# Memory sums, feed-forward preparation, key eviction and side work rearranged in a one-core decoder step

## The chip, the cores and the metric

The kernel runs on one core of a Trainium2 chip. The metric is the device time of one execution in microseconds; the kernel before takes 2075.16 us, the median of three runs.

## The reference, cut to what matters

One layer of a decoder for 1024 prompt tokens and 8 sample tokens (one for each of 8 requests). The 1032 columns run together through the dense products; only attention treats them apart.

```python
x = x + merged @ w_o                                    # conv and sparse attention branches
# memory cross-attention, 4 heads of 256; prompt: 256 memory tokens, samples: cached memory
q = rms_norm(x, g_mem) @ w_mq
p = softmax(q @ mem_k.T * 256 ** -0.5)
x = x + (p @ mem_v) @ w_mo
# feed-forward
h = rms_norm(x, g_ffn)
x = x + (silu(h @ w_gate) * (h @ w_up)) @ w_down
```

For the samples the memory keys and values differ from request to request, so their scores and weighted sums are no shared matrix product: each is a product with the query (or with the probabilities) and a sum over 256 elements.

## The kernel before, in words

Everything is kept transposed: channels on the 128 partitions, tokens on the free axis, as tiles of 128x1032. A float32 product is made of three fp32r products, high by high, high by low, low by high. So every operand is split: ScalarE makes the high part (a copy that rounds), and VectorE or GpSimd subtracts it to get the low part. Class `Weights` does this for the streamed weights (line 163 high, 165 low, on the engines named in `lo_engines`), `split_sb` (lines 499 and 502) for activations in SBUF; both use GpSimd unless told otherwise. Tiles come from 49 slots, handed out in the order in which they were given back. The order of instructions on each engine is the order of the program text; nothing is reordered.

`dense` (line 480) multiplies one output tile of 128 channels, 8 blocks of 9 matmuls, into three PSUM banks, in turn banks 0 to 2 and 3 to 5. `unit` (line 610) is a form with seven products instead of eight for a 2x2 block of tiles. Its weights, class `UnitWeights`, come in portions U, V, W and Y: `load` issues three DMAs, `sums` four additions on VectorE (lines 228 to 231), `high` a ScalarE copy (238) and `low` a VectorE subtraction (251). Its inputs come from `x_sums` (lines 550 to 563) and `x_last` (577, 578).

Ahead of the first unit two key tiles are computed with `dense` and copied out of PSUM on ScalarE (line 908). After the first of them the weights of unit 0 and two `x_sums` are prepared.

The memory stage. Eight `dense` steps give the eight query tiles. `evict_q` takes each out of PSUM (line 1571 on VectorE), keeps its sample columns (1572) and splits it. Beside this runs side work, one generator `mem_sample` for each of the four heads, started after query tiles 1, 3, 5 and 7. It spreads a head's sample query over the partitions (1620, 1624, 1626), forms the products with the cached keys in four parts (`products`), sends the 16 sums through DRAM (`bounce`) to come back as one row for a request, applies the softmax (1632 to 1636), spreads the probabilities (1639, 1641), forms the products with the cached values, bounces again and writes the sample columns (1649 to 1655). `bg.pump(budget)` advances the generators: each yields a cost, and a pump goes on until its budget is used or the generator yields None. Steps for TensorE are held until `bg.pe`.

Then a loop of eight steps, n = 0 to 7, does the prompt's softmax for (head, half of the queries). In its order: eviction of the output of step n-2 (`mo_evict`: ScalarE 1751 and VectorE 1752, twice), `ms_exp(n+1)` (four exponentials on ScalarE, 1703), the scores of n+2 (1684), held side work for TensorE, transposes (1717), `ms_norm(n+1)` (a reciprocal on VectorE, 1708, and four multiplications on GpSimd, 1711), the values of n-1 (1741), the high part of the transposed probabilities (ScalarE, 1723), `ms_max(n+2)` (VectorE, 1695 and 1696), their low part (VectorE, 1727), and one pump of budget 0.5. In step 6 the exponentials stand ahead of the eviction. The output product w_mo follows in `residual_gemm`, in two halves of eight `dense(4, ...)`: the first half pumps 3.5 after each and then drains the side work, the second half adds up squares and splits the result (499, 504, 1532, 1536).

The feed-forward part begins with two hidden tiles by `dense` (`FF_DIRECT`), gate and up each, with `x_sums` between, then goes on with units. Line 1872 evicts a gate tile, 1873 is its sigmoid, line 662 the multiplications, 1887 evicts an up tile.

Of the kernel before, what the change touches and what calls it, by code (L numbers as in the profile page):

```python
# [13 lines left out]
ALU = mybir.AluOpType  # L14
# [310 lines left out]
def build(tc, A):  # L325
# [28 lines left out]
    def store(dst, src, slot=None):  # L354
        def go():
            nc.sync.dma_start(dst, src)
            if slot is not None:
                S.put(slot)
        later.append(go)
# [540 lines left out]
    for g in range(2):  # L900
        ps = dense(8, h, 0.0, {k: score for k in range(8)} if g == 0 else None)
        if g == 0:
            score()
            for t in iq:
                S.put(t)
            put_pairs([ik])
        t = S.get()
        ACT.activation(full(t), ps, AF.Copy)
        V.tensor_copy(ks_new[:, g, :], t[0][:, 0:NS])
        store(A["o_kT"][g], act(t), t)  # L910
        if g == 0:
            UW.sums(0)
            UW.high(0, "U")
            UW.low(0, "U")
            for p in (2, 3):
                x_sums(h, None, p, xs[2 * p], xs[2 * p + 1])
            UW.high(0, "V")
            UW.low(0, "V")
            UW.high(0, "W")
    x_last(h)  # L920

    bias = {}
# [593 lines left out]

    x1d = dram.tile([8, 128, T], F32, name="x1d")

    def residual_gemm(src, xsrc, gi, spill, budget=0.0, hooks=None, free=True):
        xx = [load(xsrc[0])]  # L1520
        hl = []
        acc = [None]
        for kh in range(2):
            for o in range(8):
                if kh == 0 and o < 7:
                    xx.append(load(xsrc[o + 1]))
                ps = dense(4, src[4 * kh:4 * kh + 4], budget, hooks if kh == 0 and o == 0 else None)
                V.tensor_tensor(full(xx[o]), ps, full(xx[o]), op=ALU.add)  # L1528
                if kh == 1:
                    hl.append(split_sb(xx[o], scale=gain(gi, o)))  # L1530
                    s = S.get()
                    ACT.activation(s[0][:, :T], xx[o][0][:, :T], AF.Square)
                    if o == 0:
                        acc[0] = s
                    else:
                        G.tensor_tensor(acc[0][0][:, :T], acc[0][0][:, :T], s[0][:, :T], op=ALU.add)
                        S.put(s)
                    if spill is not None:
                        store(spill[o], xx[o][0][:, :T], xx[o] if free else None)
            put_pairs(src[4 * kh:4 * kh + 4])  # L1540
            bg.drain()
            budget = 0.0
        return xx, hl, acc[0]
# [19 lines left out]
    qlast = []  # L1563

    def split_q(t):
        qm.append(split_sb(t))
        S.put(t)

    def evict_q(o, ps, now=True):
# [23 lines left out]
    def products(src, hd, rows, dst):  # L1593
        for part in range(4):
            n = xjobs.index((src, hd, part))
            fetch(n + 1)
            s = xtiles.pop((src, hd, part))
            for x in range(4):
                V.tensor_tensor_reduce(out=caus, in0=s[0][:, 256 * x:256 * x + 256], in1=rows, scale=1.0, scalar=0.0,  # L1599
                                       op0=ALU.mult, op1=ALU.add, accum_out=dst[:, 4 * part + x:4 * part + x + 1])  # L1600
                if x < 3:
                    yield 0.46
            S.put(s)
            fetch(n + 1 + xahead[0])
            if part < 3:
                yield 0.46

    def bounce(hd, z, src, dst):
        def go():
            nc.sync.dma_start(bd[hd, z], src)  # L1610
            nc.sync.dma_start(dst, bd[hd, z].rearrange("(b g) j -> b (g j)", g=16))
        later.append(go)

    def mem_sample(hd):
        P = PS[:, 6 + hd // 2, 256 * (hd % 2):256 * (hd % 2) + 256]
        s = S.get()
        t = s[0]
        rep, rows, sums, p = t[:, 0:256], t[:, 256:512], t[:, 512:528], t[0:NS, 528:784]
        for x in range(2):
            V.tensor_copy(rep[:, 128 * x:128 * x + 128].rearrange("p (b r) -> p b r", r=16),  # L1620
                          qm_s[:, 2 * hd + x, :].unsqueeze(2).to_broadcast([128, NS, 16]))
        yield PE_STEP
        for x in range(2):
            PE.transpose(P[:, 128 * x:128 * x + 128], rep[:, 128 * x:128 * x + 128], ident)
        yield None
        ACT.copy(rows, P)
        yield None
        yield from products("cmk", hd, rows, sums)
        bounce(hd, 0, sums, p)
        yield None  # L1630
        m = sm[:, hd, :]
        V.reduce_max(m[:, 0:1], p, axis=AX.X)
        V.tensor_scalar(m[:, 1:2], m[:, 0:1], -SCM, None, op0=ALU.mult)
        ACT.activation(p, p, AF.Exp, bias=m[:, 1:2], scale=SCM, accum_out=m[:, 2:3])
        V.reciprocal(m[:, 3:4], m[:, 2:3])
        V.tensor_scalar(p, p, m[:, 3:4], None, op0=ALU.mult)
        yield None
        yield PE_STEP
        PE.matmul(P, sel128, p, start=True, stop=True)
        yield None  # L1640
        ACT.copy(rows, P)  # L1641
        yield None
        yield from products("cmv", hd, rows, sums)
        bounce(hd, 1, sums, p)
        yield None
        yield None
        yield PE_STEP
        for x in range(2):
            PE.transpose(P[:, 8 * x:8 * x + 8], p[:, 128 * x:128 * x + 128], ident[0:NS, 0:NS])
        yield None  # L1650
        for x in range(2):
            ACT.copy(qm[2 * hd + x][0][0][:, 0:NS], P[:, 8 * x:8 * x + 8])
        for x in range(2):
            h, l = qm[2 * hd + x]
            V.tensor_tensor(l[0][:, 0:NS], P[:, 8 * x:8 * x + 8], h[0].bitcast(F32)[:, 0:NS], op=ALU.subtract)
        S.put(s)
        done.add(hd)

    done = set()

    ps0 = dense(8, hl, hooks={7: h0})
    ps1 = dense(8, hl, hooks={5: h1})
    evict_q(0, ps0)
# [101 lines left out]
        raws.append(raw)  # L1765

    def split_mkv(z):
        (mkr if z < 2 else mvr).append(split_sb(raws[z], width=1024))
        S.put(raws[z])

    def mem_start():
# [36 lines left out]
    for n in range(8):  # L1808
        flush()
        if n == 3:  # L1810
            W.load_to(W.cur + 3)
        if n == 5:
            W.split_to(W.cur + 1)
        if n >= 2 and n != 6:
            mo_evict(n - 2)
        if n + 1 < 8:
            ms_exp(n + 1, range(4))
        if n == 6:
            mo_evict(n - 2)
        if n + 2 < 8:  # L1820
            ms_mm(n + 2, range(4))
        if n > 0:
            bg.pe()
        mt_mm(n)
        if n + 1 < 8:
            ms_norm(n + 1)
        bg.consume()
        if n == 0:
            split_mkv(2)
            split_mkv(3)  # L1830
        if n >= 1:
            mpv(n - 1)
        mt_hi(n)
        if n + 2 < 8:
            ms_max(n + 2)
        mt_lo(n)
        if n == 0:
            split_mkv(1)
        if n == 1:
            split_q(qlast.pop())  # L1840
        bg.pump(SLOT_SIDE, False)
    put_pairs(mkr)

    def finish_mem():
        mo_evict(6)
# [8 lines left out]

    W.limit = W.n - sum(len(g) for g in FF_GROUPS)
    flip[0] = 1
    xx, hl, sq = residual_gemm(qm, x1d, GFFN, x2d, 3.5, {1: finish_mem}, False)
    R, h0, h1 = norm_hooks(sq)
    Rr = R[0][:, :T]

    kept = {}
    tail = [{}]

    UW.n = A["wu"].shape[0]
    UW.load(MIX_UNITS)
    for f in FF_DIRECT:
        pg = dense(8, hl, hooks=None if f else {7: h0})
        x_sums(hl, GFFN, 2 * f, xx[4 * f], xx[4 * f + 1])
        if f == 0:
            pu = dense(8, hl, hooks={5: h1})  # L1870
        t, z = S.get(), S.get()
        V.tensor_tensor(full(t), pg, full(R), op=ALU.mult)
        ACT.activation(act(z), act(t), AF.Sigmoid)  # L1873
        mul(act(t), Rr)
        mul(act(t), act(z))
        S.put(z)
        if f == 0:
            UW.sums(MIX_UNITS)
            UW.high(MIX_UNITS, "U")
            UW.low(MIX_UNITS, "U")  # L1880
        else:
            UW.high(MIX_UNITS, "V")
            UW.low(MIX_UNITS, "V")
            UW.high(MIX_UNITS, "W")
            pu = dense(8, hl)
        x_sums(hl, GFFN, 2 * f + 1, xx[4 * f + 2], xx[4 * f + 3])
        V.tensor_tensor(full(t), pu, full(t), op=ALU.mult)  # L1887
        store(fd[f], act(t), t)
    x_last(hl)
    xx = []  # L1890
    for p in range(len(FF_DIRECT) // 2, 11):
# [11 lines left out]
        last = {}  # L1903
        if p == 10:
            def begin_down():
                W.limit = W.n
                W.load_to(W.cur + 2)
                xx.extend(load(x2d[o]) for o in range(4))
# [255 lines left out]
```

## Time and profile before

| what | value |
|---|---|
| median of three runs | 2075.16 us (2074.7 to 2077.28) |
| the profiled execution | 2075.18 us |
| its span, first to last instruction | 2073.4 us |
| TensorE matmul busy | 2037.3 us, 98% |
| VectorE busy | 1236.9 us, 60% |
| ScalarE busy | 821.6 us, 40% |
| GpSimd busy | 402.5 us, 19% |
| mean granted TensorE clock | 0.997 |

PE is TensorE, DVE VectorE, ACT ScalarE, POOL GpSimd. The profiled execution lies 1.8 us over its span, and 0.02 us over the median, so a change of the span can be put on the median as it is. TensorE is busy nearly throughout; what can be won is its waits, so the views to read are those that name what ended them.

### The profile page before, as it was taken

Reading aid. Unit: us, or ns where it says so; the run is one execution under the profiler, and the core shown is the slowest. Engines: PE = TensorE matmul, PEld = TensorE weight load, DVE = VectorE, ACT = ScalarE, POOL = GpSimd, SP = SyncE. Lnnn points to the kernel's source line nnn. Section 1 sums busy time; section 2 is a strip of 40 time slices with the busy share of each in tenths; the row PEclk is TensorE's granted clock in tenths of the full one; section 3 lists DMA queues with packets and bytes.
Section 4 is the critical chain, followed back from the end, with each engine's and each line's share of the span. In section 5 each row is a group of like instructions: output and inputs, shape, how many; then the busy total and the mean of one; then the engine's idle time right before and its main releaser. Section 6 shows DMA issues by size and latency. Waiting matters only on the chain. (4 is left out here: it accounts for less than half of the span.)

```text
span 2073.4 us, 35037 instructions
## 1 busy us (share of the span) xinstructions
PE 2037.3 (98%) x14455; PEld 1972.7 (95%) x14455; DVE 1236.9 (60%) x2174; ACT 821.6 (40%) x1326; POOL 402.5 (19%) x307
## 2 busy tenths in 40 slices
PE   8999999999999999999999999999999999999998
PEld 7999999999999987889999989999999999999997
DVE  6757677779866346852234787467677677721114
ACT  4437667775324235751122252343222222321204
POOL 0000000000001233333434352420000000274404
PEclk9999999999999999999999999999999999999999
DMA  7212312121327540053324424312221321453102
GB/s 297 87 42 83 123 42 82 62 82 52 135 93 265 179 141 29 1 194 94 131 92 148 181 101 164 116 38 73 85 78 62 103 82 62 166 192 103 51 1 82
DMA packets 79873, 217.48 MB, mean 105 GB/s; under 512 B 9690, under 2 KB 24354, under 8 KB 79714
## 3 DMA queue, kind: packets, MB, share of 16 engines
q1 hardware_dynamic: 79170, 214.73, 29.6%
q8 instruction: 113, 1.85, 0.4%
q10 hardware_dynamic: 544, 0.53, 0.1%
q14 instruction: 46, 0.38, 0.1%
HBM read 167.28 MB, written 47.94 MB: 104 GB/s over the span
## 5 line engine op out<-in xcount | busy, mean ns | idle before, releaser
L610 PE MATMUL PS<-t,t 128*128 128x258 f32 x7392 | 893.8, 283 | 7.3 <-DVE t L1887 3.2
L610 PEld LDWEIGHTS PS<-t,t 128*128 128x128 f32 x7392 | 890.8, 189 | 10.2 <-DVE t L1887 3.4
L480 PE MATMUL PS<-t,t 128*128 128x344 f32 x4824 | 769.1, 320 | 3.1 <-DVE t L165 1.3
L480 PEld LDWEIGHTS PS<-t,t 128*128 128x128 f32 x4824 | 760.7, 188 | 7.1 <-issue 1.7
L165 POOL TENSOR_TENSOR t<-t,t 128x1024 fp32r<-128x1024 f32 x66 | 160.8, 2446 | 354.9 <-ACT t L163 326.5
L251 DVE TENSOR_TENSOR t<-t,t 128x1024 fp32r<-128x1024 f32 (+1 forms) x176 | 188.8, 1086 | 6.4 <-ACT t L238 6.4
L238 ACT ACTIVATE t<-t 128x1024 fp32r<-128x1024 f32 (+1 forms) x176 | 161.7, 947 | 68.8 <-DVE t L228 60.8
L948 ACT ACTIVATE PS<-t,cand 128x1024 f32<-128x1024 f32 (+4 forms) x160 | 144.0, 900 | 55.6 <-DVE cand L955 52.5
L1967 DVE TENSOR_TENSOR t<-PS,t 128x1032 f32<-128x1032 f32 x32 | 39.5, 1233 | 163.1 <-PE PS L480 163.1
L531 POOL TENSOR_TENSOR t<-t,t 128x1032 fp32r<-128x1032 f32 x22 | 53.7, 2454 | 416.1 <-ACT t L530 401.5
L662 DVE TENSOR_TENSOR t<-t,t 128x1032 f32<-128x1032 f32 (+1 forms) x100 | 114.0, 1149 | 2.8 <-ACT t L1873 2.3
L163 ACT ACTIVATE t<-t 128x1024 fp32r<-128x1024 f32 x79 | 82.3, 1051 | 72.8 <-PE PS L480 60.9
L616 DVE TENSOR_TENSOR t<-PS,t 128x516 f32<-128x516 f32 x44 | 30.6, 695 | 108.8 <-PE PS L610 108.1
L499 ACT ACTIVATE t<-t 128x1032 fp32r<-128x1032 f32 (+2 forms) x34 | 36.0, 1067 | 142.2 <-DVE t L1511 77.1
L614 ACT COPY t<-PS 128x516 f32<-128x516 f32 x44 | 25.9, 589 | 164.8 <-PE PS L610 164.6
L1528 DVE TENSOR_TENSOR t<-PS,t 128x1032 f32<-128x1032 f32 x32 | 39.4, 1232 | 79.6 <-PE PS L480 79.6
L1599 DVE CUSTOM_DVE_ANT_0 caus<-t,t 128x256 bf16<-128x256 f32 x128 | 78.7, 615 | 10.3 <-ACT t L1641 5.3
L502 POOL TENSOR_TENSOR t<-t,t 128x1032 fp32r<-128x1032 f32 (+1 forms) x22 | 53.5, 2438 | 109.4 <-ACT t L499 91.5
L619 ACT COPY t<-PS 128x516 f32<-128x516 f32 x26 | 15.4, 592 | 144.5 <-PE PS L610 144.5
L1220 POOL TENSOR_SCALAR t<-t,ast 128x128 f32<-128x128 f32 (+7 forms) x64 | 48.1, 752 | 120.2 <-DVE ast L1219 88.0
L530 ACT ACTIVATE t<-t 128x1032 fp32r<-128x1032 f32 x40 | 41.4, 1060 | 74.1 <-PE PS L480 46.8
L1239 DVE TENSOR_TENSOR t<-PS,t 128x512 fp32r<-128x512 f32 x72 | 49.6, 688 | 32.1 <-ACT t L1235 31.4
(269 smaller groups left out, 2017.5 us busy)
## 6 DMA issues: line engine op xcount, KB each, us to landing
t<-in_ws_dram SPq DMA_DIRECT2D x86, 512.0 KB, 4.9
t<-in_wu_dram SPq DMA_DIRECT2D x44, 512.0 KB, 4.1
t<-in_wu_dram SPq DMA_DIRECT2D x88, 256.0 KB, 5.4
fd<-t SPq DMA_DIRECT2D x18, 516.0 KB
t<-fd SPq DMA_DIRECT2D x18, 516.0 KB, 11.5
t<-in_xT_dram SPq DMA_DIRECT2D x16, 516.0 KB, 8.1
t<-in_cmk_dram SPq DMA_DIRECT2D x16, 512.0 KB, 5.4
t<-in_cmv_dram SPq DMA_DIRECT2D x16, 512.0 KB, 6.0
```

The costliest lines, as they stand in the source:

```text
L163: nc.scalar.activation(h[0][:, :1024], raw[0][:, :1024], AF.Copy)
L165: eng.tensor_tensor(l[0][:, :1024], raw[0][:, :1024], h[0].bitcast(F32)[:, :1024], op=ALU.subtract)
L238: self.nc.scalar.activation(h[0][:, :w], self.raw[u][x][0][:, :w], AF.Copy)
L251: self.nc.vector.tensor_tensor(l[0][:, o:o + w], raw[0][:, :w], h[0].bitcast(F32)[:, :w], op=ALU.subtract)
L480: PE.matmul(PS[:, b + c, :CH], w, x[0][:, c * CH:(c + 1) * CH], start=(k == 0 and p == 0), stop=(k == n - 1 and p == 2))
L502: (lo or G).tensor_tensor(l[0][:, :width], src[0][:, :width], hf, op=ALU.subtract)
L531: lo.tensor_tensor(l[0][:, a:b], raw[0][:, a:b], h[0].bitcast(F32)[:, a:b], op=ALU.subtract)
L610: PE.matmul(PS[:, banks[z] + c, :HC], a, b[:, HC * c:HC * c + HC], start=j < 3 and q == 0 and p == 0 or j == 5 and q == 0 and p == 0, stop ...
L662: V.tensor_tensor(o, o, i, op=ALU.mult)
L948: ACT.activation(wide[:, :128 * (i + 1)], sc[i], AF.Sign, bias=candf[:, n:n + 1], scale=-1.0, accum_out=tval[:, n:n + 1])
L1239: V.tensor_tensor(tl[0][:, :512], PS[:, t_bank(x), :], th[0].bitcast(F32)[:, :512], op=ALU.subtract)
L1599: V.tensor_tensor_reduce(out=caus, in0=s[0][:, 256 * x:256 * x + 256], in1=rows, scale=1.0, scalar=0.0, op0=ALU.mult, op1=ALU.add, accum_o ...
```

## The change

- `products`: a part of 128x1024 was four instructions on VectorE, each a product and a sum over 256 columns. Now one VectorE multiplication makes all four products in place, and four ScalarE copies with an accumulating output make the sums. The costs yielded go from 0.46 for each of four to 0.9 for each half of a part. The sums go to `ast`, a tile of their own.
- `bounce` yields None until its two DMAs have been issued; `mem_sample` yields once more after its exponential.
- The low parts of the query tiles, of the memory keys and values, and of the weights from w_mq to the end of the softmax loop move from GpSimd to VectorE. So do the weights of the second half of w_mo and of the first feed-forward tiles; the first half of w_mo and w_down stay on GpSimd.
- In the softmax loop, from n = 1 on, there are two pumps of 0.5 at the end of a step; the last query tile is split in step 3 instead of 1.
- The portions V and W of unit 0 are prepared after both key tiles are evicted.
- The first feed-forward unit is loaded, summed and split (U, V) inside the second half of w_mo, after its tiles 2, 4, 5 and 6; W is prepared in the second hidden tile. The first up tile is evicted ahead of the second `x_sums`.

```diff
@@ first unit
-            UW.high(0, "V")
-            UW.low(0, "V")
-            UW.high(0, "W")
+    UW.high(0, "V")
+    UW.low(0, "V")
+    UW.high(0, "W")
     x_last(h)
@@ residual_gemm, second half
                         store(spill[o], xx[o][0][:, :T], xx[o] if free else None)
+                    if after and o in after:
+                        after[o]()
@@ split_q, and split_mkv likewise
-        qm.append(split_sb(t))
+        qm.append(split_sb(t, lo=V))
@@ products
+            v = s[0][:, :1024].rearrange("p (x n) -> p x n", n=256)
+            V.tensor_tensor(v, v, rows.unsqueeze(1).to_broadcast([128, 4, 256]), op=ALU.mult)
+            yield 0.9
             for x in range(4):
-                V.tensor_tensor_reduce(out=caus, in0=s[0][:, 256 * x:256 * x + 256], in1=rows, scale=1.0, scalar=0.0,
-                                       op0=ALU.mult, op1=ALU.add, accum_out=dst[:, 4 * part + x:4 * part + x + 1])
-                if x < 3:
-                    yield 0.46
+                ACT.activation(v[:, x, :], v[:, x, :], AF.Copy, accum_out=dst[:, 4 * part + x:4 * part + x + 1])
             S.put(s)
             fetch(n + 1 + xahead[0])
             if part < 3:
-                yield 0.46
+                yield 0.9
@@ bounce
         later.append(go)
+        while (hd, z) not in sent:
+            yield None
@@ softmax loop
         mt_lo(n)
+        if n:
+            bg.pump(SLOT_SIDE, False)
         if n == 0:
             split_mkv(1)
-        if n == 1:
+        if n == 3:
             split_q(qlast.pop())
         bg.pump(SLOT_SIDE, False)
@@ feed-forward
-    xx, hl, sq = residual_gemm(qm, x1d, GFFN, x2d, 3.5, {1: finish_mem}, False)
+    xx, hl, sq = residual_gemm(qm, x1d, GFFN, x2d, 3.5, {1: finish_mem}, False,
+                               {0: lows_on_vector, 2: lambda: UW.load(MIX_UNITS), 4: lambda: UW.sums(MIX_UNITS),
+                                5: lambda: first_part("U"), 6: lambda: first_part("V")})
...
         V.tensor_tensor(full(t), pu, full(t), op=ALU.mult)
+        if f == 0:
+            x_sums(hl, GFFN, 2 * f + 1, xx[4 * f + 2], xx[4 * f + 3])
```

## Rows read from the trace of the kernel before

**Rows 1.** Waits of PE, whole run: line <- releaser: us, times, longest

```profile
PE PS L1684 <- ACT t L1641: 2.1, 1, 2.1
```

**Rows 2.** Waits of PE, 1200 to 1270 us (first and last of six)

```profile
PE PS L1741 <- DVE t L1752: 1.9, 1, 1.9
...
PE PS L1717 <- POOL t L1711: 0.3, 1, 0.3
```

**Rows 3.** Windows: stretch, length, busy us (x instructions) by engine, granted clock, DMA, GB/s

```profile
1196.00:1248.00 52.00, 48.80 (x327) 43.98 (x327) 44.49 (x87) 33.65 (x93) 25.45 (x35) 1.00 0.27 101
...
1193.00:1196.00 3.00, 3.00 (x16) 3.00 (x16) 2.83 (x11) 0.00 (x0) 0.78 (x1) 0.50 0.19 76
...
1400.00:1406.00 6.00, 2.78 (x24) 2.58 (x23) 5.50 (x8) 4.41 (x9) 0.00 (x0) 1.00 0.00 0
```

**Rows 4.** Timeline before the first unit: start, us, instruction, xcount [idle before <-releaser]

```profile
166.94 1.99 ACT L238 ACTIVATE t<-t 128x1024 fp32r<-128x1024 f32 x2
...
168.84 1.01 ACT L908 ACTIVATE t<-PS 128x1032 f32<-128x1032 f32 x1
...
169.90 2.31 PE L610 MATMUL PS<-t,t 128*128 128x258 f32 x17 [2.16 <-ACT t L908]
```

**Rows 5.** Timeline, one step of the softmax loop

```profile
1223.38 3.05 PE L1684 MATMUL PS<-t,t 128*128 128x256 f32 x24
...
1225.61 1.04 ACT L1751 CAST t<-PS 128x512 fp32r<-128x512 f32 x2
...
1227.26 3.06 PE L1741 MATMUL PS<-t,t 128*128 128x512 f32 x12
...
1228.65 1.19 DVE L1695 TENSOR_REDUCE mst<-PS 128x4 f32<-128x1024 f32 x1
...
1229.88 0.44 DVE L1696 TENSOR_SCALAR mst<-mst 128x4 f32<-128x4 f32 x1
...
1230.16 2.04 PE L1684 MATMUL PS<-t,t 128*128 128x256 f32 x16
1230.22 1.21 DVE L1727 TENSOR_TENSOR t<-PS,t 128x1024 fp32r<-128x1024 f32 x1
...
1232.16 1.28 DVE L1752 TENSOR_TENSOR t<-PS,t 128x512 fp32r<-128x512 f32 x2
```

**Rows 6.** The chain of work that ended last, same step: start, us, what

```profile
1226.65 1.82 ACT t L1703 x8
```

**Rows 7.** Groups of ScalarE by shape: xcount | busy us, mean ns | idle before

```profile
L163 ACT ACTIVATE t<-t 128x1024 fp32r<-128x1024 f32 x79 | 82.3, 1051 | 72.8 <-PE PS L480 60.9 <-DMA t<-in_ws_dram 10.7 <-PE PS L610 0.7
...
L2001 ACT ACTIVATE t<-t 128x258 f32<-128x258 f32 x8 | 3.4, 422 | 8.6 <-DVE t L1996 8.6
...
L1634 ACT ACTIVATE t<-t,sm 8x256 f32<-8x256 f32 x4 | 2.0, 512 | 9.5 <-DVE sm L1633 9.5
```

**Rows 8.** Timeline, a low part of 1024 columns on VectorE

```profile
140.62 1.23 DVE L165 TENSOR_TENSOR t<-t,t 128x1024 fp32r<-128x1024 f32 x1
```

**Rows 9.** Timeline, side work on VectorE beside GpSimd

```profile
1180.58 2.47 POOL L502 TENSOR_TENSOR t<-t,t 128x1024 fp32r<-128x1024 f32 x1 [1.17 <-ACT t L499]
...
1180.87 2.48 DVE L1599 CUSTOM_DVE_ANT_0 caus<-t,t 128x256 bf16<-128x256 f32 x1
...
1183.38 0.42 DVE L1599 CUSTOM_DVE_ANT_0 caus<-t,t 128x256 bf16<-128x256 f32 x1
```

**Rows 10.** Timeline, start of the feed-forward part

```profile
1375.74 2.50 DVE L662 TENSOR_TENSOR t<-t,t 128x1032 f32<-128x1032 f32 x2 [1.13 <-ACT t L1873]
...
1381.83 0.69 DVE L550 TENSOR_TENSOR t<-t 128x516 f32<-128x516 f32 x1
...
1386.68 1.23 DVE L1887 TENSOR_TENSOR t<-PS,t 128x1032 f32<-128x1032 f32 x1
...
1388.06 11.73 PE L480 MATMUL PS<-t,t 128*128 128x344 f32 x72 [1.15 <-DVE t L1887]
...
1405.89 19.28 PE L610 MATMUL PS<-t,t 128*128 128x258 f32 x158 [3.22 <-DVE t L1887]
```

More of the change, by code (lines that the diff above doesn't have):

```diff
@@ L1517, in build, with residual_gemm @@
     x1d = dram.tile([8, 128, T], F32, name="x1d")
-    def residual_gemm(src, xsrc, gi, spill, budget=0.0, hooks=None, free=True):
+    def residual_gemm(src, xsrc, gi, spill, budget=0.0, hooks=None, free=True, after=None):
         xx = [load(xsrc[0])]
@@ L1605, in products @@
             if part < 3:
-                yield 0.46
+                yield 0.9
+    sent = []
     def bounce(hd, z, src, dst):
@@ L1611, in go @@
             nc.sync.dma_start(dst, bd[hd, z].rearrange("(b g) j -> b (g j)", g=16))
+            sent.append((hd, z))
         later.append(go)
+        while (hd, z) not in sent:
+            yield None
     def mem_sample(hd):
@@ L1617, in mem_sample @@
         t = s[0]
-        rep, rows, sums, p = t[:, 0:256], t[:, 256:512], t[:, 512:528], t[0:NS, 528:784]
+        rep, rows, p = t[:, 0:256], t[:, 256:512], t[0:NS, 528:784]
+        sums = ast.rearrange("p a b -> p (a b)")[:, 16 * (hd % 2):16 * (hd % 2) + 16]
         for x in range(2):
@@ L1628, in mem_sample @@
         yield from products("cmk", hd, rows, sums)
-        bounce(hd, 0, sums, p)
-        yield None
+        yield from bounce(hd, 0, sums, p)
         m = sm[:, hd, :]
@@ L1634, in mem_sample @@
         ACT.activation(p, p, AF.Exp, bias=m[:, 1:2], scale=SCM, accum_out=m[:, 2:3])
+        yield None
         V.reciprocal(m[:, 3:4], m[:, 2:3])
@@ L1643, in mem_sample @@
         yield from products("cmv", hd, rows, sums)
-        bounce(hd, 1, sums, p)
-        yield None
+        yield from bounce(hd, 1, sums, p)
         yield None
@@ L1659, in build @@
     done = set()
+    W.lo_engines = [V]
     ps0 = dense(8, hl, hooks={7: h0})
@@ L1767, in split_mkv @@
     def split_mkv(z):
-        (mkr if z < 2 else mvr).append(split_sb(raws[z], width=1024))
+        (mkr if z < 2 else mvr).append(split_sb(raws[z], lo=V, width=1024))
         S.put(raws[z])
@@ L1842, in build @@
     put_pairs(mkr)
+    W.lo_engines = [G]
     def finish_mem():
@@ L1856, in build, with first_part, lows_on_vector @@
     flip[0] = 1
-    xx, hl, sq = residual_gemm(qm, x1d, GFFN, x2d, 3.5, {1: finish_mem}, False)
+    UW.n = A["wu"].shape[0]
+    def first_part(x):
+        UW.high(MIX_UNITS, x)
+        UW.low(MIX_UNITS, x)
+    def lows_on_vector():
+        W.lo_engines = [V]
+    xx, hl, sq = residual_gemm(qm, x1d, GFFN, x2d, 3.5, {1: finish_mem}, False,
+                               {0: lows_on_vector, 2: lambda: UW.load(MIX_UNITS), 4: lambda: UW.sums(MIX_UNITS),
+                                5: lambda: first_part("U"), 6: lambda: first_part("V")})
     R, h0, h1 = norm_hooks(sq)
@@ L1862, in build @@
     tail = [{}]
-    UW.n = A["wu"].shape[0]
-    UW.load(MIX_UNITS)
     for f in FF_DIRECT:
@@ L1876, in build @@
         S.put(z)
[L1877 to L1883, printed above, removed]
+        if f:
             UW.high(MIX_UNITS, "W")
             pu = dense(8, hl)
-        x_sums(hl, GFFN, 2 * f + 1, xx[4 * f + 2], xx[4 * f + 3])
+            x_sums(hl, GFFN, 2 * f + 1, xx[4 * f + 2], xx[4 * f + 3])
         V.tensor_tensor(full(t), pu, full(t), op=ALU.mult)
+        if f == 0:
+            x_sums(hl, GFFN, 2 * f + 1, xx[4 * f + 2], xx[4 * f + 3])
         store(fd[f], act(t), t)
@@ L1905, in begin_down @@
             def begin_down():
+                W.lo_engines = [G]
                 W.limit = W.n
```

## The prediction, made before the changed kernel was run

> **What bounds the kernel now.** I read the busy line first: TensorE is at 98%, so the change can only move TensorE's waits. The view of waits, filtered to TensorE, says what ended them: 2.1 us ahead of the first memory scores [rows 1], 3.9 us in six waits of the softmax loop and just behind it [rows 2], 2.16 us in the first unit [rows 4], and 1.15 and 3.22 us at the start of the feed-forward part [rows 10]. That is 12.5 us, to which the windows add one stretch of 3 us at clock 0.50, 1.2 GHz, right after the 2.1 us wait [rows 3]; nearly all the gain to be had lies here. Then I read the timeline of each place, for what the late engine does before it comes to the instruction that TensorE awaits.
>
> **The change part by part.** *Key eviction.* Before the second key tile leaves PSUM (L908), ScalarE splits V and W: 1.99 us in one row [rows 4]. The second product of the unit needs the banks. Moved behind it, the two splits lie beside TensorE's second product, and V is needed one product (2.9 us) later than that. L908 comes some 1.8 us sooner: -1.8. If ScalarE's later work, the same in sum, becomes late, it is nothing: 0 to -1.9.
>
> *First feed-forward tiles.* Before, VectorE ran sums, a low part and an `x_sums` (1381.83 to 1386.68, 4.85 us) ahead of the eviction of the first up tile [rows 10]. After, that eviction follows the multiplications that end at 1378.2, and ends at 1379.4, when TensorE still works on the second gate tile, until 1386.9 (1388.06 less the wait); the 1.15 us go. Behind it VectorE has an `x_sums` (to 1384.3), a weight low part, new here (1.23 [rows 8], to 1385.5), an `x_sums` (1390.4), gate eviction 1.23, sigmoid 1.07, multiplications 2.5 (1395.2), an `x_sums` (1400.0) and the second eviction (1401.3). TensorE, 1.15 us sooner, ends its first product at about 1401.5 (1405.89 less both waits); so next to nothing is left of 3.22. Together -4.2. The moved portions (three DMAs on SP, four sums, two splits on each engine) go into the second half of w_mo, where VectorE has 2.5 us of work in a step of 5.7 and a PSUM bank waits one more step; the DMAs are issued two tiles (11 us) ahead of the sums. I cost them at nothing; if GpSimd's squares hold VectorE up there, it comes to -2.5.
>
> *Query tiles.* Without GpSimd, no instruction of VectorE stands 2.48 us instead of 0.42 beside it [rows 9]. But ScalarE now has the sums. For one sum no row is exact. Below is the plain 258-column activation, 0.42, whose accumulator read overlaps to about 0.41 from start to start; above is the 256-column one with a bias operand, 0.51 [rows 7]. The sums have no such operand, so I take 0.41: 1.65 a part, 2.05 at the upper end. ScalarE has four parts (6.6) and a memory split ahead of the last query tile's split; VectorE's low parts wait for those in order, and TensorE's wait of 2.1 shrinks to about 1. The clock's fall behind it (3 us at half speed: 1.5) may go with it. The two low parts ahead of head 2's spread sample query cost 0.4. Together -2.2, bounds -3.5 to +2.
>
> The Trainium skill, "ScalarE: Activation LUTs", section "Rules for kernel authors", says to add on VectorE rather than ScalarE, and budgets about 0.3 us an ACTIVATE with a bias operand and 0.83 ns an element: 0.51 for one sum, an estimate, 2.05 for four. The row with a bias operand agrees; by it the steady step below would be 0.4 us longer.
>
> *Softmax loop.* Here the order of the text decides. The multiplication stands on VectorE behind maxima and low part; the four sums stand on ScalarE behind it, and ahead of the next step's evictions and exponentials. So the two engines form a ring; before, ScalarE ran ahead, as the side work had none of its instructions. One turn: two eviction copies 1.04, exponentials 1.82 [rows 5, 6], reciprocal with waits 0.18 (from the exponentials' end to the maxima's start), maxima 1.19, negation 0.44 beside GpSimd, low part 1.21 [rows 5], multiplication 1.23 (priced as a low part of two SBUF tiles [rows 8]), sums 1.65: 8.76 us. TensorE's step, scores to scores, is 6.78 [rows 5]: 2.0 us wait a step, at the values, which need the bank that the eviction frees. By the side work's order (costs of 0.9, two pumps of 0.5) each step from 1 to 7 has one part. The waits:
> - values of unit 1: about 1, where 1.9 was;
> - values of unit 2: 2.0;
> - scores of unit 6 (step 4): they need the low part of the last query tile, which in step 3 now stands behind the multiplication. From the eviction's start 1.04+1.82+0.18+1.19+0.44+1.21+1.23+1.23 = 8.3; TensorE starts its values at 1.2 and ends them at 4.1: 4.2;
> - step 5: two multiplications, the weight split now on both engines and the evictions (1.28 on VectorE) come ahead of head 2's L1639, which needs bank 7. From those scores on, 12.8 against TensorE's 2.9+1.0+2.9+2.9 = 9.7: 3.1;
> - step 6: the exponentials stand ahead of the eviction, so head 1's L1649 waits for a turn and another 1.82: 10.0 against 4.6: 5.4;
> - the first half of w_mo, bank of the last values: 1.2.
>
> That is 16.9 for 3.9 [rows 2]: +13.0. With sums at 0.51 it is +16; if half of it hides in gaps that I don't see, +6.5. The bounce's extra yields and the SP queue behind them cost no wait of their own; they only push head 1's side work from step 2 to step 4, which is in the list.
>
> Sum: -1.8 - 4.2 - 2.2 + 13.0 = +4.8. The profiled execution took 2075.18 us (span 2073.4 and 1.8 around it), which is the median of the runs too: 2080.0.
>
> **The rivals.** *The ring doesn't bind (faster).* Before, VectorE is the fuller of the two in the loop, 44.5 of 52 us against 33.7 [rows 3]; if its hold-ups beside GpSimd make all of the waits, and the sums fit into ScalarE's pockets, the loop's waits fall from 3.9 to about 1: -1.8 - 4.2 - 2.2 - 2.9 = -11, 2064. It decides at a turn under 6.78. Against it: that 2.0 us would have to go, and the sums alone are 1.65. Chance 0.15. The Trainium skill, "Perfetto Trace Analysis", section "Optimizing Scalar/DVE Operations", is on its side: it advises offloading work to Scalar where DVE is saturated. Rows 3 show the room that it means; no row shows the order that I count against it.
>
> *The ring binds, but for half (same).* Where one long wait lets the late engine catch up, the next is smaller than listed. +6.5 in the loop gives -1.7, 2073.5; +10 gives 2077. For it: before, single waits of the loop are followed by ones under 0.5. Against it: the ring has no slack to catch up in. Chance 0.34.
>
> *More than that (slower).* Sums at 0.51 add 3 us in the loop and 1.6 in the query tiles, and waits of 3 to 5 us may bring the clock to half again, as after 2.1 us, though not after 3.22 [rows 3], 1.5 us each: 2088. Chance 0.13.
>
> **How the numbers follow.** My forecast, 2080.0, has the remaining 0.38, for 2076 to 2084. A measurement of this kernel can tell about 0.2% (4.2 us) from no change. Slower by more than that (over 2079.3): 0.13 and most of 0.38, together 0.47. Faster (under 2071): 0.16, the first rival and the edge of the second. Within: 0.37. The range, 2067 to 2090, leaves out most of the first rival and the far end of the third.
>
> **What would show it.** The key part: TensorE's wait at L908 under 0.5 us. Feed-forward: no TensorE wait on L1887 above 0.5. The ring: in the loop TensorE waits for L1752 and for the last query tile's low part, ScalarE waits some 2 to 3 us a step for the multiplication, and steps are near 8.8 us apart; a part's sums take 1.6 to 2.1. I am wrong if ScalarE's evictions come before the multiplication's end, or if steps stay near 6.8; and if the feed-forward waits stay, VectorE was too late in the second half of w_mo.

## The result, and where the time went

The changed kernel takes 2087.9 us, the kernel before 2077.2 beside it: ratio 1.0052, 95% interval 1.0041 to 1.0063, or +10.7 us. The profiled execution has a span of 2086.1 us, 12.7 over that of before. Lines from 1601 on have moved; a line of after is named with that of before in brackets. Four lines recur: L1760 (1752) is VectorE's part of an eviction in the softmax loop, which frees the PSUM bank of a unit's values; L502 is the low part of the last query tile; L1662 (1655) is VectorE's low part of head 0's sample columns; L1528 adds w_mo's product to the residual and so frees its bank. The waits of TensorE in the changed kernel (line <- releaser: us, times, longest):

```profile
PE PS L1656 <- DVE t L1760: 5.2, 1, 5.2
PE PS L1647 <- DVE t L1760: 3.5, 1, 3.5
...
PE PS L1692 <- DVE t L502: 2.8, 1, 2.8
PE PS L480 <- DVE t L1528: 2.4, 1, 2.4
PE PS L1749 <- DVE t L1760: 2.3, 2, 1.8
PE PS L1692 <- DVE t L1662: 2.1, 1, 2.1
...
PE PS L610 <- DVE t L1902: 0.3, 1, 0.3
PE PS L1725 <- DVE t L1735: 0.3, 1, 0.3
PE PS L610 <- ACT t L908: 0.3, 1, 0.3
```

Against [rows 1, 2, 4, 10]: at the key eviction (L908) 2.16 fell to 0.3. At the start of the feed-forward part 1.15 and 3.22 fell to 0.3 (L1902, before 1887), but 2.4 us for L1528 came in the second half of w_mo. Ahead of the first scores (L1692, before 1684) 2.1 stayed 2.1, though another instruction ends it: L1662, where before it was L1641, a copy of another head's probabilities. The softmax loop is what cost: L1749 2.3 (1741), L1692 2.8, L1647 3.5 (1639), L1656 5.2 (1649) and L1725 0.3 make 14.1 us where 3.9 were [rows 2]. The timeline shows one turn of the ring that the prediction describes:

```profile
1222.17 0.42 ACT L1604 ACTIVATE t<-t 128x256 f32<-128x256 f32 x1 [3.17 <-DVE t L1601]
...
1222.59 0.40 ACT L1604 ACTIVATE t<-t 128x256 f32<-128x256 f32 x1
...
1223.78 1.04 ACT L1759 CAST t<-PS 128x512 fp32r<-128x512 f32 x2
...
1226.09 0.48 ACT L1711 ACTIVATE t<-PS,mst 128x256 f32<-128x256 f32 x1
...
1226.76 0.18 DVE L1716 RECIPROCAL mst<-mst 128x4 f32<-128x4 f32 x1 [1.10 <-ACT t L1711]
1226.86 1.20 DVE L1703 TENSOR_REDUCE mst<-PS 128x4 f32<-128x1024 f32 x1
...
1228.36 1.21 DVE L1735 TENSOR_TENSOR t<-PS,t 128x1024 fp32r<-128x1024 f32 x1
...
1229.49 1.21 DVE L1601 TENSOR_TENSOR t<-t,t 128x1024 f32<-128x1024 f32 x1
...
1230.73 0.42 ACT L1604 ACTIVATE t<-t 128x256 f32<-128x256 f32 x1 [2.21 <-DVE t L1601]
```

The first of ScalarE's sums (L1604) waits 3.17 us for VectorE's multiplication (L1601); the evictions (L1759) stand behind the sums, the exponentials (L1711) behind those, and VectorE's reciprocal (L1716), maxima, low part and next multiplication behind the exponentials. From the first sum to the next step's first is 1222.17 to 1230.73, 8.56 us, where TensorE has 6.78 of work [rows 5].

A second cost stands in the windows behind the two longest waits (stretch, length, busy us (x instructions) of PE, PEld, DVE, ACT, POOL, granted clock, DMA share, GB/s):

```profile
1244.00:1248.00 4.00, 3.53 (x12) 2.78 (x13) 2.14 (x4) 1.50 (x6) 1.85 (x4) 0.52 0.88 323
1248.00:1252.00 4.00, 3.96 (x12) 2.77 (x10) 2.10 (x2) 0.63 (x1) 0.00 (x0) 0.63 1.01 381
...
1256.00:1260.00 4.00, 2.85 (x12) 2.71 (x13) 1.61 (x5) 1.58 (x5) 1.85 (x4) 0.50 0.44 178
1260.00:1264.00 4.00, 4.00 (x20) 3.32 (x19) 2.36 (x2) 1.58 (x6) 0.00 (x0) 0.85 0.76 270
```

A granted clock of 0.50 is 1.2 GHz; these stretches lie at it or partly at it. Busy time by the missing share of the clock (3.53x0.48 + 3.96x0.37 + 2.85x0.50 + 4.00x0.15) makes an estimate of 5.2 us. The half-speed stretch of before, behind the first scores' wait [rows 3], is absent.

A third shows on SP. Its costliest wait from 1160 to 1262 (us in total, times, longest), its timeline (DMA issues; the length of a row with several is from first to last), and the multiplication that came after:

```profile
SPq L1614 <- ACT t L1604: 46.2, 2, 40.4
```

```profile
1241.04 0.33 SPq L1614 DMA_DIRECT2D bd<-ast  x1
1242.48 0.30 SPq L1615 DMA_DIRECT2D t<-bd  x1
1242.87 1.28 SPq L1591 DMA_DIRECT2D t<-in_cmk_dram  x3
1244.21 10.23 SPq L1591 DMA_DIRECT2D t<-in_cmv_dram  x7
```

```profile
1251.12 1.23 DVE L1601 TENSOR_TENSOR t<-t,t 128x1024 f32<-128x1024 f32 x1 [1.23 <-DMA t<-in_cmv_dram]
```

The copy of the sums to DRAM (L1614) waits 40.4 us at the head of SP's queue for ScalarE's last sum, and ten loads of cached keys and values stand behind it. The multiplication of step 5 waits 1.23 us for one of them.

The terms: key -1.9, feed-forward -1.5 (4.4 to 0.3, and 2.4 and 0.2 new), the slow stretch behind the first scores -1.5, waits in the loop +10.2, slow clock +5.2: +10.5. Another 1.6 us lie between the rows that start at 763.85 and 785.88 (22.0 us here, 20.4 before), where this execution shows clock 0.92; the stretch is in the profile of e3 below and not in that of e6, which are the same up to there, so it is not the change's. Together that is 12.1 of the 12.7 us between the spans; the rest is not assigned.

### The profile page after: what moved, and what is told of

It reads as the page before. It is cut to its first block, busy times and chain, and to the rows that moved or that the text cites. A ratio compares the mean times of both kernels' runs of the same rounds, so it can differ in the third digit from the quotient of the medians.

```text
span 2086.1 us, 35034 instructions
## 1 busy us (share of the span) xinstructions
PE 2043.6 (98%) x14455; PEld 1976.4 (95%) x14455; DVE 1228.7 (59%) x1976; ACT 872.3 (42%) x1582; POOL 339.8 (16%) x281
## 5 line engine op out<-in xcount | busy, mean ns | idle before, releaser
L165 POOL TENSOR_TENSOR t<-t,t 128x1024 fp32r<-128x1024 f32 x52 | 125.6, 2423 | 323.5 <-ACT t L163 295.3
L1528 DVE TENSOR_TENSOR t<-PS,t 128x1032 f32<-128x1032 f32 x32 | 39.4, 1230 | 75.3 <-PE PS L480 72.2
L1197 PE MATMUL PS<-t,t 128*128 128x512 f32 (+3 forms) x288 | 67.0, 359 | 1.0 <-DVE ast L1205 1.0
L1604 ACT ACTIVATE t<-t 128x256 f32<-128x256 f32 x128 | 51.5, 404 | 36.4 <-DVE t L1601 30.5
```

Source lines behind the costliest of these rows:

```text
L165: eng.tensor_tensor(l[0][:, :1024], raw[0][:, :1024], h[0].bitcast(F32)[:, :1024], op=ALU.subtract)
L1197: PE.matmul(PS[:, b + c // 512, :w], u[0][:, cs], y[0][:, NS + c:NS + c + w], start=pp == 0, stop=pp == 2)
L1604: ACT.activation(v[:, x, :], v[:, x, :], AF.Copy, accum_out=dst[:, 4 * part + x:4 * part + x + 1])
```

## The experiments

All times are medians, with the kernel before run beside them (2076.2 to 2077.2 us from round to round), so kernels are compared by the last column.

| kernel | us | ratio to before, 95% interval | us against before |
|---|---|---|---|
| changed kernel | 2087.86 | 1.0052 [1.0041, 1.0063] | +10.7 |
| e1 ring opened | 2079.62 | 1.0014 [1.0005, 1.0024] | +3.2 |
| e2 half of the sums | 2082.07 | 1.0025 [1.0016, 1.0035] | +5.6 |
| e3 sums on VectorE | 2065.82 | 0.9944 [0.9927, 0.9960] | -10.6 |
| e4 key and feed-forward alone | 2072.47 | 0.9984 [0.9974, 0.9994] | -4.0 |
| e5 ring opened, loads early | 2070.07 | 0.9966 [0.9952, 0.9980] | -6.8 |
| e6 e3, squares on VectorE | 2063.56 | 0.9934 [0.9917, 0.9951] | -13.3 |
| e7 loads early alone | 2086.72 | 1.0043 [1.0029, 1.0057] | +9.9 |
| e8 low parts alone | 2070.06 | 0.9966 [0.9952, 0.9980] | -6.8 |
| e9 last query tile split early | 2087.30 | 1.0053 [1.0036, 1.0069] | +11.2 |
| e10 e5 with e9's and e6's edits | 2064.30 | 0.9940 [0.9923, 0.9956] | -11.9 |
| e11 e10, query splits first | 2068.63 | 0.9960 [0.9945, 0.9975] | -7.9 |
| e12 query splits first alone | 2090.83 | 1.0067 [1.0049, 1.0085] | +14.3 |

### Is it the order of the sums, or their amount? (e1, e2)

e1 moves the second pump of a step, which holds the sums, behind the next step's exponentials, and `flush`, which queues the DMAs of a bounce, with it. This is called the opened ring below.

```diff
-        flush()
...
             ms_exp(n + 1, range(4))
         if n == 6:
             mo_evict(n - 2)
+        if n:
+            bg.pump(SLOT_SIDE, False)
+        flush()
...
-        bg.pump(SLOT_SIDE, False)
+    bg.pump(SLOT_SIDE, False)
```

> The second portion of side work of a step, which holds the four sums on ScalarE, stands behind the next step's evictions and exponentials; the work is the same and nothing else moves. Theory (ring by order): ScalarE no longer waits for the multiplication ahead of the evictions; of the 16.0 us that TensorE waits in the changed loop (from the values of unit 1 to L1656) some 3 to 6 remain (the scores of unit 6, and the weight split of step 5), the two stretches at clock 0.50 go, and the time is 2070 to 2076 us. Rival (the engines are too full: four sums of 0.40 a step are too much for ScalarE wherever they stand): waits and time stay within 3 us of the changed kernel, 2085 to 2090.

The time fell by 7.5 us, to 3.2 over before: the waits at the values are gone, at L1647 3.5 fell to 0.25 and the scores' wait from 2.8 to 1.4. The rival falls: the same sums at another place in ScalarE's order cost less. But 2079.6 is over the 2076 of the theory. One wait grew, and the clock behind it is 0.50 from 1248 to 1252:

```profile
PE PS L1656 <- DVE t L1760: 8.3, 1, 8.3
```

```profile
1247.32 1.22 DVE L1601 TENSOR_TENSOR t<-t,t 128x1024 f32<-128x1024 f32 x1 [6.88 <-DMA t<-in_cmv_dram]
1248.46 1.28 DVE L1760 TENSOR_TENSOR t<-PS,t 128x512 fp32r<-128x512 f32 x2
```

VectorE came to the multiplication of step 5 earlier and now waits 6.88 us for its load; the eviction (L1760) stands behind it. SP issued those loads from 1240.5 on, behind the copy of the sums at 1237.4, 3.7 us earlier than in the changed kernel (1244.2 and 1241.0), but VectorE came to the multiplication 9.5 us earlier (1240.4 and 1249.9). The ring had hidden a second bound.

e2 keeps the order and leaves out every second sum:

```diff
-            for x in range(4):
+            for x in range(0, 4, 2):
                 ACT.activation(v[:, x, :], v[:, x, :], AF.Copy, accum_out=...)
```

> Two of the four sums of each part are left out, so half the results of the memory products are missing; the order is that of the changed kernel. Theory (ring): a turn is 0.80 us shorter, 8.56 to 7.76, so the loop's waits fall by some 4 to 6 us and part of the slow clock goes; in the query tiles ScalarE's sixteen sums become eight, 3.2 us less ahead of the key split, and the 2.1 us wait at the first scores goes to 0 to 1. In all 2078 to 2082. Rival (VectorE, with a multiplication of 1.2 where the sums were, is the bound, and the sums lie in ScalarE's free time): less than 2 us change, 2086 to 2089.

2082.1, at the top of the theory's range; the rival (under 2 us) falls. A turn is 0.8 us shorter, and so are the waits that a turn sets: the values from 1.79 to 0.97, L1647 from 3.52 to 2.27. The wait at the first scores is gone. The one at L1656 rose to 7.6; a load is late again (2.80 us of wait on VectorE).

### What each part is worth alone (e3, e4, e8)

e3 puts `products`, `bounce` and `mem_sample` of before back, takes the extra pump out and splits the last query tile in step 1; low parts, key eviction and feed-forward portions stay as changed.

```diff
-            V.tensor_tensor(v, v, rows.unsqueeze(1).to_broadcast([128, 4, 256]), op=ALU.mult)
-            yield 0.9
             for x in range(4):
-                ACT.activation(v[:, x, :], v[:, x, :], AF.Copy, accum_out=...)
+                V.tensor_tensor_reduce(out=caus, in0=..., in1=rows, ..., accum_out=...)
...
-        if n:
-            bg.pump(SLOT_SIDE, False)
...
-        if n == 3:
+        if n == 1:
             split_q(qlast.pop())
```

> Undoes the memory sums alone: products and sums in one VectorE instruction each as before, one portion a step, the last query tile split in step 1. The low parts on VectorE, the key eviction and the feed-forward portions stay as changed. Theory: the loop is as before or better (waits 3 to 4 us), key -1.9 and feed-forward -1 to -2 remain, and the lows on VectorE give between 0 and -2 in the query tiles: 2071 to 2075. Rival (the lows on VectorE, not the sums, fill that engine): the loop's waits stay over 8 us and the time over 2080.

e4 is the kernel before with the edits for the key eviction and the feed-forward part, and nothing of the memory stage:

```diff
-            UW.high(0, "V")
-            UW.low(0, "V")
-            UW.high(0, "W")
+    UW.high(0, "V")
+    UW.low(0, "V")
+    UW.high(0, "W")
     x_last(h)
...
+    xx, hl, sq = residual_gemm(qm, x1d, GFFN, x2d, 3.5, {1: finish_mem}, False,
+                               {0: lows_on_vector, 2: lambda: UW.load(MIX_UNITS), 4: lambda: UW.sums(MIX_UNITS),
+                                5: lambda: first_part("U"), 6: lambda: first_part("V")})
```

> The kernel before with the key eviction and the feed-forward portions alone; the memory stage is that of before. Theory: -1.9 at the key eviction; at the feed-forward start the two waits (1.15 and 3.22) go and a wait of 2.4 us for L1528 comes in the second half of w_mo: -1.5 to -2; together 2073 to 2074.5. Rival (the wait in w_mo comes from the memory stage's late side work and not from the portions): it is absent here, -6 in all, 2071.

e8 is the kernel before with the low parts of the memory stage on VectorE:

```diff
-        qm.append(split_sb(t))
+        qm.append(split_sb(t, lo=V))
...
+    W.lo_engines = [V]
     ps0 = dense(8, hl, hooks={7: h0})
...
-        (mkr if z < 2 else mvr).append(split_sb(raws[z], width=1024))
+        (mkr if z < 2 else mvr).append(split_sb(raws[z], lo=V, width=1024))
...
+    W.lo_engines = [G]
```

> The kernel before, with the low parts of query tiles, memory tiles and weights of the memory stage on VectorE instead of GpSimd, and nothing else. Theory (GpSimd's low parts hold VectorE in the query tiles and at the loop's start): the waits at the first scores (2.1), at the values of unit 1 (1.9) and the stretch at half clock go, -5.5 to -7: 2069 to 2071.5. Rival (the prediction's term: the wait at the first scores halves and the slow clock goes, the loop keeps its waits): -2 to -3, 2073.5 to 2074.5.

The low parts of the memory stage alone give -6.8, key and feed-forward -4.0 (0.5 us better than its theory's range), together -10.8; e3, which has both, gives -10.6. So the parts add up, and the sums on ScalarE with what came with them (two pumps, the late split, the longer bounces) cost the changed kernel 21.3 us; e3 takes these out together, so it does not part them. In e8 the waits at the first scores (2.1) and at the first values (1.9) are not merely halved but gone, and the clock behind the first is 1.00:

```profile
1192.00:1196.00 4.00, 4.00 (x34) 4.00 (x33) 3.62 (x9) 1.27 (x6) 0.00 (x0) 1.00 0.00 0
```

e8's theory held and its rival, which is the prediction's own term, fell. e3 was better than expected by 5 us for the same reason. In e4 the 2.4 us wait for L1528 is there (2.37), so it comes from the feed-forward edit and not from late side work.

### The second bound (e5, e7)

One line ahead of the loop issues three loads of cmk and two of cmv before the copy of the sums is queued (e5 on top of e1, e7 on the changed kernel):

```diff
     xahead[0] = XAHEAD
+    fetch(26)
```

> The opened ring of the run before, and five loads (three of cmk, two of cmv) issued at the loop's start instead of behind the copy of the sums to DRAM (L1614), which waits on SP's queue for ScalarE's last sum until 1237.4. Theory (second bound, SP's order): VectorE's multiplication of step 5, which waited 6.88 us for its load, waits under 1; the 8.3 us ahead of L1656 fall to under 2.5 and clock 0.74 behind it goes: 2069 to 2074. Rival (the wait at L1656 is the bank's, which the last eviction frees late in step 6 whatever loads do): it stays over 5 us, 2077 or more.

> The changed kernel and the five loads at the loop's start alone; the ring stays. Theory (ring first, SP's order behind it): the 1.2 us that step 5's multiplication waits for its load go, and the wait at L1656 falls from 5.2 to about 4; the others stay: 2085 to 2087. Rival (late loads are the cause of the long waits): L1647 and L1656 fall under 1.5 both, and the time to 2077 to 2080.

With the ring opened (e5) the line is worth 9.9 us: L1656 falls from 8.3 to 1.5 and the clock stays at 1.00 from 1240 to 1264. With the ring closed (e7) it is worth 0.8 us, less than the intervals can tell from nothing; the two long waits stay:

```profile
PE PS L1656 <- DVE t L1760: 3.7, 1, 3.7
PE PS L1647 <- DVE t L1760: 3.2, 1, 3.2
```

Both theories held. Some of e7's gain is hidden by the clock: its waits in the loop are 11.5 us, 2.6 fewer than in the changed kernel, but its profile has a clock of 0.84 and 0.73 from 1228 to 1236, where the changed kernel's has 1.00, and by the same estimate as above the slow clock costs it about 7.3 us and not 5.2. So the ring comes first and hides most of what the loads cost; neither edit alone brings back more than 7.5 us, both together 17.5.

### Does the late split cost by itself? (e9, e10)

```diff
-        if n == 3:
+        if n == 1:
             split_q(qlast.pop())
```

> The changed kernel, with the last query tile split in step 1 as before and not in step 3. Theory: the 2.8 us wait of the scores of unit 6 goes, but in a ring ScalarE's split (1.06) and VectorE's low part (1.22) only move to step 1, and the later steps still need a turn of 8.6 each, so less than the 2.8 comes back: 2084.5 to 2087. Rival (a wait of its own, that adds to the ring's): the whole 2.8 goes, and with it the waits behind it start earlier by as much: 2083 to 2084.5 or less.

Nothing that the intervals can tell came back: 2087.3. The scores' wait of 2.8 is gone, but its place in the ring is taken by the values, three waits instead of two, and the later ones are longer:

```profile
PE PS L1656 <- DVE t L1760: 5.6, 1, 5.6
PE PS L1647 <- DVE t L1760: 4.9, 1, 4.9
PE PS L1749 <- DVE t L1760: 4.2, 3, 1.9
```

The evictions L1759 start at 1214.14, 1222.72 and 1231.35, 8.6 apart whatever TensorE waits at. The time is just over the theory's range and far from the rival's. It says that these entries of the prediction's list tell where the ring's time is booked and are not separate costs.

e10 takes this edit, e5's and e6's (below) together.

> Sums on ScalarE with all causes found so far taken out: the sums behind the next step's exponentials, five loads at the loop's start, the last query tile split in step 1, squares added on VectorE. Theory: of the waits only that at the first scores (2.0, sixteen sums ahead of the key split on ScalarE) and about 1.5 at L1656 remain, and a stretch at half clock behind the first of them: 2066 to 2068, slower than the 2063.6 with VectorE sums by the query tiles' wait and clock. Rival (sums on ScalarE relieve VectorE where it now waits for nothing, and are worth something once the ring is open): 2063 or less.

2064.3: better than the theory's 2066, and not under the rival's 2063. With the ring open, sums on ScalarE come within 1.4 us of sums on VectorE (e6), which the intervals can't part, and no better, though the 2.0 us wait at the first scores, clock 0.68 behind it and 1.5 us at L1656 are still there.

### Who is late in the second half of w_mo? (e6)

```diff
-                        G.tensor_tensor(acc[0][0][:, :T], acc[0][0][:, :T], s[0][:, :T], op=ALU.add)
+                        (V if after else G).tensor_tensor(acc[0][0][:, :T], acc[0][0][:, :T], s[0][:, :T], op=ALU.add)
```

> The kernel with VectorE sums, and the squares of w_mo's second half added up on VectorE instead of GpSimd. Theory (GpSimd holds up VectorE): the low parts there take 1.2 us instead of 2.75 and the first addition of the feed-forward sums 0.7 instead of 2.9, so though VectorE has seven additions of 1.2 more, the 2.4 us wait for L1528 falls to under 0.6: -1.5 to -2.4 against the kernel with VectorE sums, 2063 to 2065. Rival (VectorE has too much work in that step, whoever works beside it): the wait grows to 3 to 5 us, 2066 to 2069.

The theory held: the wait for L1528 is gone and the time is 2063.6, the lowest of all kernels here, 13.3 us under before. Timelines of e3 and then e6, the same low part of a weight (L165):

```profile
1310.75 2.57 POOL L1536 TENSOR_TENSOR t<-t,t 128x1032 f32<-128x1032 f32 x1 [11.37 <-ACT t L1532]
1311.65 2.75 DVE L165 TENSOR_TENSOR t<-t,t 128x1024 fp32r<-128x1024 f32 x1 [0.61 <-ACT t L163]
```

```profile
1308.43 1.22 DVE L1536 TENSOR_TENSOR t<-t,t 128x1032 f32<-128x1032 f32 x1
1309.57 1.22 DVE L165 TENSOR_TENSOR t<-t,t 128x1024 fp32r<-128x1024 f32 x1
```

Beside GpSimd's addition of squares the low part takes 2.75 us and ends 1.1 us after GpSimd does; without it 1.22. The first of the feed-forward additions (L228) goes from 2.90 to 0.68. VectorE got seven additions more and was earlier. The Trainium skill, "SBUF — State Buffer", section "Who interferes with whom", says that a DVE instruction with two SBUF inputs contends with a GpSimd instruction that reads SBUF, and that the order of issue decides which one blocks. The rows agree: GpSimd's addition started 0.9 us ahead, and the low part is the one that was held.

### The query tiles (e11, e12)

e12 puts the side work that followed `dense` of query tile 6 behind that tile's split and the key tile's (e11 does the same in e10):

```diff
-        if o < 7:
+        if o < 6:
             bg.pump(4.5)
...
         evict_q(o, ps, o < 7)
+        if o == 6:
+            bg.pump(4.5)
```

> The run with all causes taken out, and in the query tiles the key tile's split and the eviction and split of query tile 6 placed ahead of the four parts of side work instead of behind them. Theory (sixteen sums of 0.40 on ScalarE ahead of these splits make the wait at the first scores): the 2.05 us wait falls to under 0.7 and the stretch at clock 0.68 behind it goes, 2061 to 2063. Rival (the loads, for which VectorE's multiplications waited 1.65 and 0.68 us, set the end there): the wait stays over 1.5, 2064 to 2065.

> The same move in the query tiles, made to the changed kernel alone. Theory: the wait at the first scores falls from 2.1 to under 0.7, and since the ring's turns count from the loop's start, the loop keeps its 14 us: 2085 to 2086.5. Rival (the ring absorbs it, as it did with the split of the last query tile): the wait goes, but the loop's grow by as much: 2087 to 2088.5.

Neither run came out by its theory or its rival: e12 is 3.6 us slower than the changed kernel, e11 3.9 slower than e10. The wait at the first scores grew, from 2.1 to 4.2 in e12 and from 2.0 to 3.8 in e11. In e12 the clock behind it is 0.61 from 1192 to 1196, worth 1.5 us by the estimate above, and with the 2.1 us of wait that is the 3.6; the loop kept its 14.0 us, as the theory said. Its timeline:

```profile
1188.69 1.20 DVE L1601 TENSOR_TENSOR t<-t,t 128x1024 f32<-128x1024 f32 x1
1189.93 0.42 ACT L1604 ACTIVATE t<-t 128x256 f32<-128x256 f32 x1 [2.87 <-DVE t L1601]
...
1191.54 0.20 ACT L1659 CAST t<-PS 128x8 fp32r<-128x8 f32 x2
...
1191.78 0.24 DVE L1662 TENSOR_TENSOR t<-PS,t 128x8 fp32r<-128x8 f32 x2 [1.88 <-ACT t L1659]
```

The scores of unit 0 go into PSUM bank 6, in which head 0's sample results lie, so they wait until these are copied out (L1659, L1662), and not for the splits. Those copies stand behind the side work and behind the splits, in either order. A part's multiplication and sums that had stood ahead of the splits now stood between them and those columns. That the sums on ScalarE make this wait in the changed kernel is shown by e2 and e3, where half of them are left out or all are on VectorE and it is gone; that it would go by putting the splits first was wrong.

## Why the prediction was right or wrong

The sign, the place and the chief mechanism were right: slower, in the softmax loop, by a ring of ScalarE and VectorE. +4.8 was forecast, +10.7 came, inside the range of 2067 to 2090 but above the 2076 to 2084 that the forecast itself stood for. The 2087.9 lies at the third rival's 2088, and of that rival's two causes one came (the slow clock) and one did not (sums at 0.51). Term by term the measured kernel differs from the sum by -0.1 (key), +2.7 (feed-forward), +0.7 (query tiles), -2.8 (the loop's waits) and +5.2 (the loop's clock, which the sum put at nothing). That the feed-forward's and the loop's waits cancel is luck.

*Key eviction.* -1.8 forecast, the wait fell by 1.9. Right.

*Feed-forward start.* -4.2 forecast. The two waits fell by 4.1 as listed, but the portions, costed at nothing in the second half of w_mo, brought 2.6 back: -1.5. The failed step is "VectorE has 2.5 us of work in a step of 5.7": those 2.5 are the addition and the low part of an output tile, and leave out the weights' low parts, which the change moves to VectorE there as well. Beside GpSimd's squares each of these stands 2.75 us, not the 1.23 of a row without GpSimd [rows 8], and the first of the moved sums 2.90. The condition was named in the same part (GpSimd's squares holding VectorE), priced at -2.5, and e6 shows that it is the cause.

*Query tiles.* -2.2 forecast: the wait to shrink from 2.1 to about 1, and the slow clock to go. The wait stayed at 2.1, since what TensorE waits for is not the low parts, as the prediction has it, but head 0's sample columns behind them (e12); the clock held in this execution, but not in those of e5, e9 and e10 with the same wait, so that part is luck and not the change's. Two terms lay in it, both too small: the low parts alone give -6.8 (e8), since they free the loop as well, and the ScalarE sums take the query tiles' share of it back. Rows 9 showed such hold-ups of 2.48 against 0.42; I counted them in the query tiles alone, though the 1.9 us wait of the loop in rows 2 had the same cause: in e8 it is gone.

*Softmax loop.* The turn was forecast at 8.76 and measured at 8.56, sums at 0.40 to 0.42 against 0.41. The 0.51 that was estimated from the Trainium skill, "ScalarE: Activation LUTs", section "Rules for kernel authors", is not what the runs show. The 0.41 was right, but not by the row it names: L2001 has no accumulator to read, and the runs, not rows 7, show that the read is hidden. The waits, forecast and measured: values of unit 1 about 1 and 0.48; unit 2 2.0 and 1.79; scores of unit 6 4.2 and 2.8; step 5 3.1 and 3.5; step 6 5.4 and 5.2; w_mo's bank 1.2 and none. 16.9 forecast, 14.1 measured (with 0.3 at L1725): too much by 2.8, mostly at the scores of unit 6 (1.4) and at w_mo's bank (1.2).

*Clock.* The step that missed most. Stretches at half clock stood in the third rival, at 1.5 us for each wait, with a chance of 0.13. They came behind L1647 and L1656 and cost an estimated 5.2, so a term that the sum put at nothing was its largest miss. The rows of before left it open: rows 3 show a fall behind a wait of 2.1 and none behind one of 3.22 (their window ends 0.1 us behind that wait; from 1406 to 1410 the clock is 1.00 as well). The list held three waits of 3 us and more, so the term could have stood in the sum, weighted by a chance.

*SP.* "The bounce's extra yields and the SP queue behind them cost no wait of their own" is wrong as a statement of causes, for the loads behind the copy of the sums made 2.6 us of the waits; in time it was nearly right, 0.8 us (e7). With the ring opened it would have been 9.9 (e5).

The rivals: that the ring doesn't bind is refuted by turns of 8.56 us, by e1 and by e9. That half of it hides is not refuted by the waits: its bounds for the loop were +6.5 and +10, and they came at +10.2. What it lacked is the slow clock. The Trainium skill's advice to offload to Scalar where DVE is saturated ("Perfetto Trace Analysis", "Optimizing Scalar/DVE Operations") has no gain to show in these runs: e10, with the order put right, is no faster than e6.

What stays open: how much slower e10 is than e6. In the two profiles TensorE idles 2.4 us more in e10, and the spans differ by 2.7, but by medians it is 0.7 to 1.4, and e6's profiled execution is its fastest. Open too is whether an order that puts head 0's sample columns ahead of other heads' sums would take the first scores' wait away; that wasn't tried.

## What to carry to other kernels

Work that goes from one in-order engine to another is priced by where it stands in the second engine's order: if it waits there for the first, and the first waits later in the same step for what stands behind it, the step becomes the sum of both (8.56 us here, for 6.78 of TensorE's), and free time on either doesn't shorten it. Where a loop is such a ring, taking out one of its waits can move the time to the next (e9); put the handed-over work one step later instead, and look at once for the next bound behind it, a DMA queue above all. The duration of a VectorE instruction where GpSimd rests isn't its duration beside GpSimd: here 1.22 and 2.75 us for the same low part.

## What the runs showed of the hardware that I had not expected

The same wait of 1.9 to 2.2 us at the first scores is followed by TensorE at half clock in some kernels' executions (0.50 before, 0.60 in e5, 0.57 in e9, 0.68 in e10) and by full clock in others (the changed kernel, e1, e4, e7), at the same place and ahead of the same matmuls. The 2.8 us wait at the scores of unit 6 is followed by 1.00 in the changed kernel and e12 and by 0.73 in e7 and 0.50 in e2. A wait of that size is a risk of about 1.5 us, not a sure cost. Behind the waits at L1647 and L1656, 3.2 to 5.6 us, the clock fell each time (the changed kernel, e7, e9, e12); behind the 3.2 us wait at the start of the feed-forward part it stayed at 1.00 (before, e8). So the length of the wait alone did not decide it.

Accumulating ScalarE copies of 256 columns start 0.40 us apart, though a row is 0.40 to 0.42 and the read of the accumulator behind it another 0.19: the read is hidden under the next copy.
